# Order in which the first projection's sums are finished and read, their PSUM banks, and VectorE's order around the first attention scores, in a decoder layer on one core

## The chip, the core and the metric

The kernel runs on one core of one Trainium2 chip. The core has TensorE (PE; its weight loads are shown apart as PEld), VectorE (DVE), ScalarE (ACT), GpSimd (POOL) and SyncE (SP), which here only issues DMA transfers. Each engine works through its own queue in order and waits on semaphores of the others. Matmul results land in PSUM, which has eight banks; a 128x512 float32 tile fills one. The metric is the time of one execution in microseconds on the device; lower is better.

## The reference, cut to what matters

One layer of a decoder with 512 tokens and 1024 channels, all in float32:

```python
shift1, scale1, gate1, shift2, scale2, gate2 = split(silu(c) @ w_ada + b_ada, 6)
h = rmsnorm(x, norm1_g) * (1 + scale1) + shift1
qa, ka, va, qd, kd, vd, ga, gd = split(h @ w_in)          # 512, 128, 128, 512, 512, 512, 1024, 1024 columns
out_a = sliding_window_attention(qa, ka, va, sinks)       # 8 heads of 64, 2 key heads, window 128
out_d = differential_attention(qd, kd, vd)                # 4 heads
merged = sigmoid(ga) * (out_a @ w_branch_swa) + sigmoid(gd) * (out_d @ w_branch_diff)
x = x + gate1 * (merged @ w_out)
x = x + gate2 * conv_ffn(rmsnorm(x, norm2_g) * (1 + scale2) + shift2)
out = rmsnorm(x, final_g)
```

## The kernel before

Every operand of a matmul is split into a high part (rounded to the matmul's format by ScalarE, which also is the cast) and a low part (the rest, by VectorE). A product is three matmuls: high by high, high by low, low by high. Reading a finished sum out of PSUM, an *evacuation* (`evac`, L422), is the same pair of operations: ScalarE writes the high part, VectorE subtracts it and writes the low part. The bank is free when both have read it.

**First projection.** `mm_k(k, part)` (L323) multiplies k-tile k (of 8) of the normalised input with the 768 columns for qa, ka and va. The six sums `acc6` stand in six banks at once: 0 to 3 are the four pairs of query heads, 4 is ka, 5 is va, transposed. The banks come from tags: `f` has two, `s` three, `t` two, `v` one. Sums 0 and 1 have the two `f` banks, 2 to 4 the three `s` banks, 5 the `v` bank. Each of the three parts goes over all six sums in turn. Then the six are evacuated in the order 0 to 5 (L430 to L434), and va is transposed back by TensorE (L438) and evacuated (L441).

**Steps and fills.** After this the order of TensorE's queue is written out by hand, and TensorE is fed from two sides. `fill(n)` (L482) issues n *steps* of background projections: one step is one k-tile of one 128-column projection, three matmuls, and a projection has eight steps. The first six are q, k and v of differential heads 0 and 1 (tiles pq, pk, pw; one `f` bank each). Their weights come through `prefetch` (L477): a DMA into one of four `raw` buffers, ScalarE's cast w_h, VectorE's low part w_l (L115). `tick` counts the steps. Between the fills stand the parts of windowed attention, by pair of heads:

- `swa_scores(i, n0)` (L520): twelve matmuls into two `s` banks (sw), for two of the four query blocks, then four VectorE instructions that add the distance bias, write the scores to st and take the row maxima (L547).
- `swa_softmax(i)` (L552): negated maxima, eight exponentials on ScalarE, the row sums, and a scaling of st by VectorE (L570), first for one head of the pair, then for the other.
- `swa_transpose(i, j)` (L573): seven transposes of st into the two `t` banks (tp, L582), then evacuation to pTh and pTl.
- `swa_values(i)` (L589): the products with va, into the `v` bank.

`SWA_FILL` gives how many steps stand in each gap. The first three entries are the gaps before the first scores of pair 0, before its second scores, and after its softmax.

**Conditioning rows.** `ada_rows` (L734) computes the rest of `silu(c) @ w_ada` on VectorE, in rounds: a DMA of 512 KB into a `raw` buffer (ra) and two operations that add it, scaled, to the tile arow (L746, L748). One round is issued at every 8th step; four fill one arow.

**What sets the order.** TensorE's queue there is in the order of the text. The queues of VectorE, ScalarE, SP and POOL are ordered when the program is built, by a list planner that goes through estimated times: of the instructions that it takes to be ready it issues the one of highest priority. Priority is the order of the text; blocks in `tc.high_priority(offset=...)` move ahead by the offset. Score maxima, softmax and evacuations of tp have the offset HP = 100000, the conditioning rounds half of it. On the chip each queue keeps that order, ready or not.

Of the kernel before, what the change touches and what calls it, by code (L numbers as in the profile page):

```python
# [8 lines left out]
F32 = mybir.dt.float32  # L9
# [19 lines left out]
ST = 6  # L29
ADA_LAG = 1  # L30
ADA_EVERY = 8
ADA_START = 4
V_LAG = 13
STAT_LAG = 10
NORM_LAG = 16
SWA_FILL = (4, 2, 3, 2, 2, 2, 2, 3)
DIFF_FILL = (3, 2, 4, 2)
WARM = 14
GROUPS = ((0,), (1,), (2,), (3,), (4,), (5,), (6,), (7,))
# [13 lines left out]
def kernel(  # L53
# [170 lines left out]
    )  # L224
    nc.sync.dma_start(crow[0:66, :], conv_w[0].rearrange("t (a p) -> (t a) p", p=P))
    nc.sync.dma_start(crow[66:88, :], conv_b[0].rearrange("(a p) -> a p", p=P))
    acc6 = [fbank("a0"), fbank("a1"), sbank("a2"), sbank("a3"), sbank("a4"), vbank("a5")]
    man = ExitStack()
    man.enter_context(tc.manual_schedule(engines={nc.vector.engine, nc.scalar.engine, nc.tensor.engine}))
    cs = cpool.tile([P, 8], F32, name="cs")  # L230
# [91 lines left out]

    def mm_k(k, part):  # L323
        wh, wl = wts[k]
        lhs, rhs = ((wh, hTh), (wl, hTh), (wh, hTl))[part]
        for i in range(6):
            nc.tensor.matmul(
                acc6[i], lhs[:, i * P : (i + 1) * P], rhs[k],
                start=k == 0 and part == 0, stop=k == KT - 1 and part == 2,
            )  # L330


    def keep_warm(n):
# [93 lines left out]
            nc.scalar.activation(hi, src, AF.Copy, scale=scale)  # L427
            nc.vector.scalar_tensor_tensor(lo, src, scale, hi.bitcast(F32), ALU.mult, ALU.subtract)

    for i in range(4):  # L430
        evac(qa[:, i, 0], qa[:, i, 1], acc6[i], qsc[:, i : i + 1])
    evac(ka[:, 0], ka[:, 1], acc6[4])
    vT = ap.tile([P, S], F32, tag="tmp", bufs=2, name="vaT")
    nc.scalar.copy(vT, acc6[5])  # L434
    nc.gpsimd.memset(va.bitcast(F32), 0.0)
    pv = tbank("pva")
    for t in range(NT):
        nc.tensor.transpose(pv[:, t * P : (t + 1) * P], vT[:, t * P : (t + 1) * P], ident)  # L438
    pv3 = pv.rearrange("p (t d) -> p t d", t=NT)
    for a, cc in ((0, 0), (64, 192)):  # L440
        evac(va[:, 0, :, cc : cc + 64], va[:, 1, :, cc : cc + 64], pv3[:, :, a : a + 64])  # L441


    pcv = tbank("pcv", (P, 88))
# [37 lines left out]
    def fill(n):  # L482
        for _ in range(n):
            if not current:
                prefetch()
                if loaded:
                    wts, run = loaded.pop(0)
                    current.append(run(wts))
                    prefetch()
            if current:  # L490
                try:
                    next(current[0])
                except StopIteration:
                    current.clear()
            for e in list(later):
                e[0] -= 1
                if e[0] <= 0:
                    later.remove(e)
                    e[1]()
            tick[0] += 1  # L500
            if tick[0] >= ADA_START and tick[0] % ADA_EVERY == 0:
                next(ada, None)
# [17 lines left out]
    def swa_scores(i, n0):  # L520
        if n0 == 0:
            c = pairs[i] = Pair()
            c.mx, c.nm, c.lsum, c.es = (
                ap.tile([P, 2, NT], F32, tag=t, bufs=2, name=f"{t}{i}") for t in ("mx", "nm", "lsum", "es")
            )
            c.sb = [ap.tile([P, 2, P], F32, tag="st0", bufs=2, name=f"st{i}_0")]
            c.sb += [ap.tile([P, 2, 256], F32, tag="st", bufs=ST, name=f"st{i}_{n}") for n in range(1, NT)]
            c.pT = []
        c = pairs[i]
        sps = [sbank(f"sw{i}_{n0}_{j}", (P, 2, 256)) for j in range(2)]  # L530
        for n in (n0, n0 + 1):
            w = P if n == 0 else 2 * P
            k0 = max(0, n - 1) * P
            qs, ks = slice(n * P, (n + 1) * P), slice(k0, k0 + w)
            mm3_rows([
                (
                    sps[j][:, n - n0, :w],
                    [qa[64 * j : 64 * j + 64, i, b, qs] for b in range(2)],
                    [ka[64 * j : 64 * j + 64, b, ks] for b in range(2)],
                )  # L540
                for j in range(2)
            ])
        for n in (n0, n0 + 1):
            w = P if n == 0 else 2 * P
            for j in range(2):
                with tc.high_priority(offset=HP):
                    nc.vector.tensor_tensor_reduce(  # L547
                        c.sb[n][:, j, :w], sps[j][:, n - n0, :w], dsw[:, 256 - w : 256], 1.0, -3e38, ALU.add, ALU.max,
                        c.mx[:, j, n : n + 1],
                    )  # L550
# [183 lines left out]
    def ada_rows():  # L734
        for idx in range(4):
            for hf in range(2):
                c0 = (2 + idx) * D + hf * S
                ac = big.tile([P, S], F32, tag="sq2", name=f"arow{idx}{hf}")
                for k in range(0, KT, 2):
                    r = raw_tile([P, 2, S], f"ra{idx}{hf}_{k}")  # L740
                    nc.sync.dma_start(r, wada[k * P : (k + 2) * P, c0 : c0 + S].rearrange("(a p) n -> p a n", p=P))
                    with tc.high_priority(offset=HP // 2):
                        for a in range(2):
                            cc = cs[:, k + a : k + a + 1]
                            if k + a == 0:
                                nc.vector.tensor_scalar_mul(ac, r[:, a], cc)  # L746
                            else:
                                nc.vector.scalar_tensor_tensor(ac, r[:, a], cc, ac, ALU.mult, ALU.add)  # L748
# [46 lines left out]
    add_head(1)  # L795
    fill(SWA_FILL[0])
    swa_scores(0, 0)
    fill(SWA_FILL[1])
    swa_scores(0, 2)
    swa_softmax(0)  # L800
    fill(SWA_FILL[2])
    for i in range(SWA_PAIRS):
        more = i + 1 < SWA_PAIRS
        if more:
# [968 lines left out]
```

## Time and profile before

| | us |
|---|---|
| three runs | 717.43, 718.32, 718.40 |
| median | 718.32 |
| the profiled execution | 719.43 |
| its span from first to last instruction | 717.4 |

The span is what the views of the profile divide; about 2 us of the execution's time lie around it. The columns of the views are explained where they are shown. A row of a timeline is start and duration in us, engine, line of the kernel, operation, output and inputs, their shape, how many of them were merged into the row, and in brackets how long the engine had stood idle before it and what released it. Matmul durations overlap: from one start to the next is what a matmul costs in a row. The mean granted TensorE clock of the execution is 0.995 of full speed.

### The profile page before, as it was taken

The page shows a single profiled execution, that of the slowest core. Times are in us where ns is not written, and L with a number is a line of the kernel's source. Part 1 is how long each engine was busy: PE and PEld are TensorE (multiplying, and loading weights), DVE is VectorE, ACT ScalarE, POOL GpSimd, SP SyncE. Part 2 cuts the span into 40 slices and gives each one's busy share as a digit, 9 for nine tenths or more (in the row PEclk, how much of TensorE's full clock was granted, in tenths as well). Part 3 has the DMA queues.
Part 4 walks back from the last instruction along what each step waited for, and adds up shares of the span by engine and source line. Part 5 has one row for each costly group of instructions (what it writes and reads, how often), then busy time and mean ns, then how long its engine had stood idle before and what let it go on. Part 6 is the DMA issues. An engine that isn't in the chain of part 4 may idle for free. (4 is left out here: it accounts for less than half of the span.)

```text
span 717.4 us, 11279 instructions
## 1 busy us (share of the span) xinstructions
PE 690.6 (96%) x4187; PEld 603.1 (84%) x4187; DVE 588.9 (82%) x1125; ACT 383.6 (53%) x677; POOL 84.0 (12%) x101
## 2 busy tenths in 40 slices
PE   5998899999999999999999999999999999999995
PEld 5776788877887888888879999999999999888884
DVE  5998877887986674875379999888889899979996
ACT  4643656455554233432358665556555666655664
POOL 4000000000100110000012021111111101540300
PEclk9999999999999999999999999999999999999998
DMA  9986122534544565726817689878779738997903
GB/s 310 301 251 205 60 59 61 176 110 126 176 114 151 183 195 182 233 90 211 245 52 156 157 179 210 200 187 219 190 191 230 168 121 237 183 203 194 161 0 118
DMA packets 115863, 121.82 MB, mean 170 GB/s; under 512 B 4415, under 2 KB 93280, under 8 KB 115808
## 3 DMA queue, kind: packets, MB, share of 16 engines
q1 hardware_dynamic: 96894, 95.09, 41.7%
q0 software_dynamic: 18720, 25.73, 21.4%
q8 instruction: 33, 0.54, 0.3%
q10 hardware_dynamic: 194, 0.28, 0.1%
q14 instruction: 22, 0.18, 0.1%
HBM read 118.97 MB, written 2.11 MB: 169 GB/s over the span
## 5 line engine op out<-in xcount | busy, mean ns | idle before, releaser
L1112 PE MATMUL up<-t,m_whi 128*128 128x256 f32 x528 | 96.1, 283 | 0.0
L1112 PEld LDWEIGHTS up<-t,m_whi 128*128 128x128 f32 x528 | 82.3, 192 | 0.0
L1112 PE MATMUL up<-t,m_wlo 128*128 128x256 f32 x264 | 74.7, 283 | 0.1
L1112 PE MATMUL up<-bh,p_wlo 128*128 128x256 f32 x232 | 65.7, 284 | 0.7 <-DVE p_wlo L1055 0.7
L1112 PE MATMUL up<-bh,p_whi 128*128 128x256 f32 x232 | 65.6, 283 | 0.0
L1112 PE MATMUL up<-bl,p_whi 128*128 128x256 f32 x232 | 65.6, 283 | 0.0
L1112 PEld LDWEIGHTS up<-t,m_wlo 128*128 128x128 f32 x264 | 50.6, 192 | 0.3 <-DVE m_wlo L1055 0.3
L1112 PEld LDWEIGHTS up<-bh,p_wlo 128*128 128x128 f32 x232 | 44.4, 192 | 1.1 <-DVE p_wlo L1055 1.1
L1112 PEld LDWEIGHTS up<-bl,p_whi 128*128 128x128 f32 x232 | 44.5, 192 | 0.0
L1112 PEld LDWEIGHTS up<-bh,p_whi 128*128 128x128 f32 x232 | 44.5, 192 | 0.0
L748 DVE SCALAR_TENSOR_TENSOR arow<-ra,cs,arow 128x512 f32<-128x512 f32 x56 | 41.9, 748 | 3.0 <-DMA ra<-in_w_ada_dram 2.3
L1023 POOL DMA_DIRECT2D s<-in_w_up_dram x21 | 27.2, 1385 | 143.2 <-DMA s<-in_w_up_dram 61.0
L1055 DVE TENSOR_TENSOR m_wlo<-s,m_whi 128x1024 fp32r<-128x1024 f32 x31 | 37.8, 1220 | 2.0 <-ACT m_whi L1051 2.0
L1051 ACT CAST m_whi<-s 128x1024 fp32r<-128x1024 f32 x31 | 32.4, 1046 | 9.4 <-DVE s L1045 6.0
L1112 PE MATMUL up<-t,p_whi 128*128 128x256 f32 x176 | 32.2, 283 | 0.0
L174 POOL TENSOR_TENSOR r<-ms,mhalf 128x1 f32<-128x1 f32 (+1 forms) x16 | 13.1, 820 | 143.2 <-DVE ms L172 76.5
L678 ACT ACTIVATE sd<-sd,dmx 128x128 f32<-128x128 f32 (+3 forms) x32 | 17.8, 557 | 22.1 <-DVE dmx L676 15.3
L761 POOL DMA_DIRECT2D mod_rows<-arow x8 | 4.3, 540 | 205.2 <-ACT arow L760 205.1
L1112 PEld LDWEIGHTS up<-t,p_whi 128*128 128x128 f32 x176 | 27.4, 192 | 0.2 <-issue 0.2
L1119 ACT ACTIVATE gT<-a,cv 128x512 f32<-128x512 f32 x22 | 17.7, 813 | 17.7 <-DVE a L1154 17.3
L1051 ACT CAST p_whi<-wa 128x1024 fp32r<-128x1024 f32 x18 | 18.7, 1040 | 12.0 <-PE up L1112 9.0
L1112 PE MATMUL up<-t,p_wlo 128*128 128x256 f32 x88 | 24.9, 283 | 0.0
(485 smaller groups left out, 2119.3 us busy)
## 6 DMA issues: line engine op xcount, KB each, us to landing
ra<-in_w_ada_dram SPq DMA_DIRECT2D x32, 512.0 KB, 4.0
wa<-in_w_up_dram SPq DMA_DIRECT2D x22, 512.0 KB, 4.3
s<-in_w_up_dram SPq DMA_DIRECT2D x21, 512.0 KB, 4.9
s<-in_w_up_dram POOLq DMA_DIRECT2D x21, 512.0 KB, 7.3
adaw<-in_w_ada_dram SPq DMA_DIRECT2D x16, 512.0 KB, 5.3
w<-in_w_in_dram SPq DMA_DIRECT2D x12, 512.0 KB, 3.9
a<-in_w_up_dram SPq DMA_DIRECT2D x11, 512.0 KB, 4.9
b<-in_w_down_dram SPq DMA_DIRECT2D x10, 512.0 KB, 3.8
```

The lines of the kernel that those rows point to most:

```text
L174: nc.gpsimd.tensor_tensor(r0, ms, mhalf[:, :n], ALU.pow)
L678: nc.scalar.activation(pm[m], pm[m], AF.Exp, bias=mx[:, m : m + 1], scale=slope, accum_out=lsum[:, m : m + 1])
L748: nc.vector.scalar_tensor_tensor(ac, r[:, a], cc, ac, ALU.mult, ALU.add)
L761: nc.gpsimd.dma_start(mod_rows[idx : idx + 1, hf * S : (hf + 1) * S], row)
L1023: nc.gpsimd.dma_start(dst, upblock(*blk), accum_op=ALU.add)
L1051: nc.scalar.copy(W[J, name][0], R[J, SRC[name]])
L1055: nc.vector.tensor_sub(lo, R[J, SRC[name]], hi.bitcast(F32))
L1112: nc.tensor.matmul(o[u], w[:, k, cu], b[:, k], start=name in ("p1", "m5", "p2") and k == 0 and x == 0, stop=k == 3 and x == 2, skip_group_ ...
L1119: nc.scalar.activation(grow(j), av[J][:, u], AF.Identity, bias=cv[:, 66 + j : 67 + j], scale=cv[:, 44 + j : 45 + j])
```

## The change

- **Banks and order of the sums.** The sums are finished, and their banks taken, in the order 0, 4, 2, 5, 1, 3. Sums 0 and 1 keep `f` banks; 4, 2 and 5 (ka, query pair 2, va) have the `s` banks, and 3 (query pair 3) has the `v` bank.
- **One by one.** In the last k-tile, parts 1 and 2 are issued together for each sum.
- **Evacuation.** Sums 0, 4, 2, 5, 1 are evacuated in this order. Sum 3 and the turning of va (`turn_va`) come after the first softmax and one step.
- **VectorE's order.** `tc.issue_after(ins)` makes every instruction that its block traces on the engine of `ins` come after `ins` in that engine's queue; it adds no wait for a result. The steps between the two score groups of pair 0, and its second scores, come behind the maxima of the first scores. The softmax of pair 0, the steps around it, the evacuation of sum 3 and of va come behind the maxima of the second scores.
- **Weights.** The third weight (v of head 0) is requested in the eighth step, no longer in the first.
- **Conditioning rounds** up to step 20 lose their raised priority: those of steps 8 and 16.
- **Steps.** Of the nine steps around the first scores, 2, 2 and 5 stand in the three gaps, before 4, 2 and 3.

```diff
@@ -29,11 +29,12 @@
 ST = 6
 ADA_LAG = 1
 ADA_EVERY = 8
+ADA_EASY = 20
 ADA_START = 4
 V_LAG = 13
 STAT_LAG = 10
 NORM_LAG = 16
-SWA_FILL = (4, 2, 3, 2, 2, 2, 2, 3)
+SWA_FILL = (2, 2, 5, 2, 2, 2, 2, 3)
 DIFF_FILL = (3, 2, 4, 2)
 WARM = 14
 GROUPS = ((0,), (1,), (2,), (3,), (4,), (5,), (6,), (7,))
@@ -224,7 +225,9 @@
     )
     nc.sync.dma_start(crow[0:66, :], conv_w[0].rearrange("t (a p) -> (t a) p", p=P))
     nc.sync.dma_start(crow[66:88, :], conv_b[0].rearrange("(a p) -> a p", p=P))
-    acc6 = [fbank("a0"), fbank("a1"), sbank("a2"), sbank("a3"), sbank("a4"), vbank("a5")]
+
+    DONE = (0, 4, 2, 5, 1, 3)
+    acc6 = {i: (fbank, sbank, vbank)[(0, 0, 1, 2, 1, 1)[i]](f"a{i}") for i in DONE}
     man = ExitStack()
     man.enter_context(tc.manual_schedule(engines={nc.vector.engine, nc.scalar.engine, nc.tensor.engine}))
     cs = cpool.tile([P, 8], F32, name="cs")
@@ -322,12 +325,15 @@
 
     def mm_k(k, part):
         wh, wl = wts[k]
-        lhs, rhs = ((wh, hTh), (wl, hTh), (wh, hTl))[part]
-        for i in range(6):
-            nc.tensor.matmul(
-                acc6[i], lhs[:, i * P : (i + 1) * P], rhs[k],
-                start=k == 0 and part == 0, stop=k == KT - 1 and part == 2,
-            )
+        last = k == KT - 1
+        if last and part == 2:
+            return
+        for i in DONE:
+            for p in (1, 2) if last and part else (part,):
+                lhs, rhs = ((wh, hTh), (wl, hTh), (wh, hTl))[p]
+                nc.tensor.matmul(
+                    acc6[i], lhs[:, i * P : (i + 1) * P], rhs[k], start=k == 0 and p == 0, stop=last and p == 2
+                )
 
 
     def keep_warm(n):
@@ -427,18 +433,25 @@
             nc.scalar.activation(hi, src, AF.Copy, scale=scale)
             nc.vector.scalar_tensor_tensor(lo, src, scale, hi.bitcast(F32), ALU.mult, ALU.subtract)
 
-    for i in range(4):
+    nc.gpsimd.memset(va.bitcast(F32), 0.0)
+
+    def evac_q(i):
         evac(qa[:, i, 0], qa[:, i, 1], acc6[i], qsc[:, i : i + 1])
+
+    evac_q(0)
     evac(ka[:, 0], ka[:, 1], acc6[4])
+    evac_q(2)
     vT = ap.tile([P, S], F32, tag="tmp", bufs=2, name="vaT")
     nc.scalar.copy(vT, acc6[5])
-    nc.gpsimd.memset(va.bitcast(F32), 0.0)
-    pv = tbank("pva")
-    for t in range(NT):
-        nc.tensor.transpose(pv[:, t * P : (t + 1) * P], vT[:, t * P : (t + 1) * P], ident)
-    pv3 = pv.rearrange("p (t d) -> p t d", t=NT)
-    for a, cc in ((0, 0), (64, 192)):
-        evac(va[:, 0, :, cc : cc + 64], va[:, 1, :, cc : cc + 64], pv3[:, :, a : a + 64])
+    evac_q(1)
+
+    def turn_va():
+        pv = tbank("pva")
+        for t in range(NT):
+            nc.tensor.transpose(pv[:, t * P : (t + 1) * P], vT[:, t * P : (t + 1) * P], ident)
+        pv3 = pv.rearrange("p (t d) -> p t d", t=NT)
+        for a, cc in ((0, 0), (64, 192)):
+            evac(va[:, 0, :, cc : cc + 64], va[:, 1, :, cc : cc + 64], pv3[:, :, a : a + 64])
 
 
     pcv = tbank("pcv", (P, 88))
@@ -486,7 +499,10 @@
                 if loaded:
                     wts, run = loaded.pop(0)
                     current.append(run(wts))
-                    prefetch()
+                    if tick[0]:
+                        prefetch()
+            if tick[0] == 7:
+                prefetch()
             if current:
                 try:
                     next(current[0])
@@ -544,7 +560,7 @@
             w = P if n == 0 else 2 * P
             for j in range(2):
                 with tc.high_priority(offset=HP):
-                    nc.vector.tensor_tensor_reduce(
+                    c.last = nc.vector.tensor_tensor_reduce(
                         c.sb[n][:, j, :w], sps[j][:, n - n0, :w], dsw[:, 256 - w : 256], 1.0, -3e38, ALU.add, ALU.max,
                         c.mx[:, j, n : n + 1],
                     )
@@ -739,7 +755,7 @@
                 for k in range(0, KT, 2):
                     r = raw_tile([P, 2, S], f"ra{idx}{hf}_{k}")
                     nc.sync.dma_start(r, wada[k * P : (k + 2) * P, c0 : c0 + S].rearrange("(a p) n -> p a n", p=P))
-                    with tc.high_priority(offset=HP // 2):
+                    with tc.high_priority(offset=HP // 2) if tick[0] > ADA_EASY else ExitStack():
                         for a in range(2):
                             cc = cs[:, k + a : k + a + 1]
                             if k + a == 0:
@@ -795,10 +811,15 @@
     add_head(1)
     fill(SWA_FILL[0])
     swa_scores(0, 0)
-    fill(SWA_FILL[1])
-    swa_scores(0, 2)
-    swa_softmax(0)
-    fill(SWA_FILL[2])
+    with tc.issue_after(pairs[0].last.ins):
+        fill(SWA_FILL[1])
+        swa_scores(0, 2)
+    with tc.issue_after(pairs[0].last.ins):
+        swa_softmax(0)
+        fill(1)
+        evac_q(3)
+        turn_va()
+        fill(SWA_FILL[2] - 1)
     for i in range(SWA_PAIRS):
         more = i + 1 < SWA_PAIRS
         if more:
```

## The prediction

> **What bounds the kernel now.** I read the page first, then busy time by stage, then what TensorE waited for, and last the order of instructions on each engine in the one stage where it waited.
>
> ```profile
> span 717.4 us, 11279 instructions
> ...
> PE 690.6 (96%) x4187; PEld 603.1 (84%) x4187; DVE 588.9 (82%) x1125; ACT 383.6 (53%) x677; POOL 84.0 (12%) x101
> ```
>
> ```profile
> 60.28:72.00 11.72, 9.38 (x49) 6.76 (x49) 8.54 (x22) 3.06 (x7) 0.00 (x0) 0.85 0.72 227
> 72.00:82.20 10.20, 8.03 (x49) 5.68 (x47) 9.96 (x37) 7.33 (x24) 0.00 (x0) 1.00 0.31 104
> 82.20:135.00 52.80, 52.80 (x347) 44.75 (x347) 41.78 (x132) 31.47 (x93) 0.70 (x1) 1.00 0.27 81
> ```
>
> The columns of the second view are the stretch, its length, then busy time (and instructions) of PE, PEld, DVE, ACT and POOL, the granted clock, the DMA share and GB/s. TensorE is the bound. From 82.2 to 135 us it never rests; between 60.28 and 82.20 us, where the first projection hands over to attention, it is idle for 2.34 + 2.17 us and is granted 0.85 of its clock in the first half. The waits to 260 us say for whom it rests:
>
> ```profile
> PE sw L125 <- DVE qa L428: 1.6, 2, 1.0
> PE td L693 <- DVE sd L684: 1.6, 3, 1.1
> ...
> PE tp L582 <- DVE pTl L425: 1.2, 1, 1.2
> ...
> PE tp L582 <- DVE st L570: 1.0, 1, 1.0
> ...
> PE od L119 <- DVE aTl L425: 0.5, 1, 0.5
> PE pq L118 <- DVE qa L428: 0.5, 1, 0.5
> ...
> PE sw L125 <- DVE ka L425: 0.3, 1, 0.3
> ```
>
> Everything named qa, ka, st or pTl here lies between 60.28 and 82.20 us and ends on a DVE instruction. TensorE's own order there (start, duration, line, instruction, in brackets the idle time before it):
>
> ```profile
> 57.32 1.56 PE L327 MATMUL a<-hThB,w0l 128*128 128x512 f32 x6
> 58.72 1.56 PE L327 MATMUL a<-hTlB,w0h 128*128 128x512 f32 x6
> 60.74 0.50 PE L118 MATMUL pq<-hThA,w_h 128*128 128x512 f32 x1 [0.46 <-DVE qa L428]
> ...
> 64.97 0.33 PE L125 MATMUL sw<-ka,qa 64*128 64x128 f32 x1 [0.62 <-DVE qa L428]
> 66.29 0.32 PE L125 MATMUL sw<-ka,qa 64*128 64x128 f32 x1 [1.00 <-DVE qa L428]
> 66.89 0.84 PE L125 MATMUL sw<-ka,qa 64*128 64x128 f32 x10 [0.27 <-DVE ka L425]
> ...
> 70.15 1.59 PE L125 MATMUL sw<-ka,qa 64*128 64x256 f32 x12
> ...
> 73.94 0.96 PE L125 MATMUL sw<-ka,qa 64*128 64x128 f32 x12
> 74.82 0.50 PE L118 MATMUL pk<-hThA,w_h 128*128 128x512 f32 x1
> ...
> 77.45 1.14 PE L582 MATMUL tp<-ident,st 128*128 128x128 f32 x7 [0.97 <-DVE st L570]
> ...
> 81.18 1.01 PE L582 MATMUL tp<-ident,st 128*128 128x128 f32 x7 [1.20 <-DVE pTl L425]
> 82.13 0.97 PE L125 MATMUL sw<-ka,qa 64*128 64x256 f32 x12
> ```
>
> And VectorE's, with two rows of ScalarE behind it:
>
> ```profile
> 56.48 0.69 DVE L321 TENSOR_TENSOR hTlB<-hf,hThB 128x512 fp32r<-128x512 f32 x1
> 57.09 2.35 DVE L115 TENSOR_TENSOR w_l<-w,w_h 128x1024 fp32r<-128x1024 f32 x2
> 59.36 0.48 DVE L746 TENSOR_SCALAR arow<-ra,cs 128x512 f32<-128x512 f32 x1
> 59.93 0.75 DVE L428 SCALAR_TENSOR_TENSOR qa<-a,qsc,qa 128x512 fp32r<-128x512 f32 x1
> ...
> 63.50 0.75 DVE L748 SCALAR_TENSOR_TENSOR arow<-ra,cs,arow 128x512 f32<-128x512 f32 x1 [1.49 <-DMA ra<-in_w_ada_dram]
> ...
> 66.15 0.68 DVE L425 TENSOR_TENSOR ka<-a,ka 128x512 fp32r<-128x512 f32 x1
> ...
> 71.78 0.42 DVE L547 CUSTOM_DVE_ANT_0 st<-sw,dsw 128x256 f32<-128x256 f32 x1 [1.69 <-PE sw L125]
> ...
> 77.03 1.07 DVE L570 TENSOR_SCALAR st<-st,lsum 128x128 f32<-128x128 f32 x4
> ...
> 80.45 1.15 DVE L425 TENSOR_TENSOR pTl<-tp,pTh 128x512 fp32r<-128x512 f32 x2
> ```
>
> ```profile
> 59.21 2.42 ACT L427 ACTIVATE qa<-a,qsc 128x512 fp32r<-128x512 f32 x4 [1.83 <-PE a L327]
> ...
> 73.18 1.05 ACT L114 CAST w_h<-w 128x1024 fp32r<-128x1024 f32 x1 [4.95 <-PE pq L119]
> ```
>
> The conditioning rows (arow, L746/L748), which nobody needs for another 40 us, are interleaved with the evacuation of the projection. At 63.50 one of them stands in VectorE's queue waiting 1.49 us for its weights, with qa 2, qa 3 and ka behind it. ka, which every score needs, is done only at 66.83.
>
> **The change, step by step.** A *step* is one k-tile of a projection: three 512-wide matmuls. Six start in 1.40 us (57.32 to 58.72), 0.233 us each, so a step is 0.70 us.
>
> *Sums finished one by one.* The number of matmuls is the same. In the last k-tile the low-weight and low-activation products are issued accumulator by accumulator. That tile's 18 matmuls start at 57.32 − 1.40 = 55.92; a0 is complete after the 8th instead of the 13th, at 55.92 + 7 × 0.233 + 0.40 = 57.95 instead of 59.12, the others each 0.47 later, a3 at the old end. The 8th needs hTlB, which is ready at 57.17 and was used only at 58.72; 0.4 us of cover are left, and if they were gone the whole tail would slip by the lateness, as no other work stands between.
>
> *Evacuation.* ScalarE takes 0.57 to 0.60 us each (four in 2.42): a0 58.05, a4 58.6, a2 59.2, vaT 59.8, a1 60.4. VectorE still splits one early weight from 57.09 to 58.23 (half of the 2.35 row; the second is deferred), then has no arow in the way: a0's low part to 59.3, ka's to 59.9, a2's to 60.6, a1's to 61.6, at 0.67 and 0.60 each. The last projection matmul starts at 59.88, so the first pq can start at 60.11, on a0's bank, free since 59.3: the 0.46 goes. Two steps last until 61.5. The first scores need qa 0 (59.3), ka (59.9) and two of the three score banks, which now held a4, a2, a5 (free at 59.9, 60.6, 60.4). So 0.62 + 1.00 + 0.27 go too: together **2.35 us**, with 0.9 us of cover (61.5 − 60.6).
>
> *The clock.* Busy time of PE, granted clock, DMA share and GB/s in two smaller stretches:
>
> ```profile
> 68.30:71.70 3.40, 3.40 (x18) 0.52 0.67 188
> ...
> 76.40:82.20 5.80, 3.63 (x23) 1.00 0.54 184
> ```
>
> Right behind those three waits the clock is 0.52 for 3.40 us: 3.40 × 0.48 = **1.6 us**. Without the waits I expect none of it. The second stretch rests longer (2.17 us) and keeps 1.00, so the dip is not certain to follow or to stay away; bounds 0 and 1.6. [...]
>
> *Restarts.* A 512-wide matmul shows 0.40 to 0.50 us alone (1.56 less five starts of 0.233; the 60.74 row) against 0.233 in a row, so each of the six stops hides about 0.15 beyond its idle figure; four go: **0.6** (bounds 0 and 1.0).
>
> *First maxima ahead, and the fills moved.* Edges that only order VectorE's queue cost no instruction. The nine steps around the first two score groups are now 2, 2, 1 + 4 instead of 4, 2, 3. The maxima start when the group has ended (71.78 after 70.15 + 1.59), and the first scaled probabilities come 77.03 + 1.07 = 78.10, or 6.4 us after it. In that time TensorE had 3 + 2 steps and a score group; now 1 + 4 + 2 steps (4.9), a score group (74.82 − 73.94 = 0.88), the four value transposes (about 0.45 by the score group's pitch) and some 0.3 of switching: 6.5 us. So the 0.97 goes. The 1.20 came from pTl starting at 80.45, 1.9 us after transposes that ended at 78.59, because VectorE was still scaling the other half; as TensorE now arrives later in that chain I expect 0.3 to 0.5 left. Of 2.17 I take **1.7** (bounds 0 and 2.17). In the same place ScalarE may or may not put a 1.05 cast ahead of the exponentials again, as at 73.18: that is inside the bounds.
>
> *What is deferred.* Four conditioning rounds ran before 82.2:
>
> ```profile
> L748 DVE SCALAR_TENSOR_TENSOR arow<-ra,cs,arow 128x512 f32<-128x512 f32 x7 | 5.2, 746 | 1.5 <-DMA ra<-in_w_ada_dram 1.5
> ```
>
> Now the rounds of steps 8 and 16 lose their priority, and 24 and 32 follow them because they add to the same tile. About six of these eight operations (6 × 0.746 = 4.5 us) and a 1.2 us weight split move into the time after the second score group of pair 1. There VectorE is busy 41.78 of 52.80 us; with 5.7 more, 90%. Most fits the gaps while ScalarE does exponentials, but one operation ahead of a pTl or a score maximum makes TensorE wait up to its own 0.75. I take **−0.7** (bounds 0 and −2.5). POOL's zeroing of va moves in the text, but POOL is idle in all these stretches: nothing. One more switch between kinds of matmul: **−0.1**.
>
> On SP the third weight is asked for in the 8th step instead of the first; nothing lies between them in that queue. Its raw slot, though, and that of the first conditioning round are now held until VectorE reaches them after the second maxima, so the loads behind, above all the fifth and sixth weight (first used in steps 33 and 41), are issued later; for these see the rival of a late weight.
>
> *Sum:* 2.35 + 1.6 + 0.6 + 1.7 − 0.7 − 0.1 = **5.45 us**. The profiled execution took 719.43 us with its span of 717.4, so 2.0 lie around the span; it would become 714.0. It is 1.1 above the median of the runs, 718.32, and a saving in the middle of a stage that TensorE bounds passes through to the end whole: 718.32 − 5.45 = 712.9 us. All gains at their upper bound and no deferred cost: 2.35 + 1.6 + 1.0 + 2.17 − 0.1 = 7.0, or 711.3.
>
> **Rivals.** *The deferred rows collide (chance 0.18).* Pairs 1 to 3 have six places where TensorE waits for pTl or maxima with little room. For it: 90% load, and rounds 24 and 32 still carry a high priority. Against: between 82.2 and 135 TensorE did not wait at all. One operation ahead at each, 0.6 of its 0.75 showing: 6 × 0.6 = 3.6 in place of 0.7, a gain of 2.55: 715.8 us.
>
> *The scores still wait (0.10).* The change doesn't do what it says: ScalarE or VectorE takes a weight's cast or split between the evacuations, because the planner thinks it has the time. For it: just that happened at 57.09 and 73.18. 1.22 us less the 0.9 of cover is 0.3 of new wait, but if two such pieces come, about 1.5 us of waits and with them the clock dip stay: 5.45 − 1.5 − 1.6 = 2.35, or 716.0 us.
>
> *Slower: a weight comes late (0.09).* SP waited like this before:
>
> ```profile
> SPq L464 <- DVE w_l L115: 16.8, 2, 16.1
> ```
>
> ```profile
> w<-in_w_in_dram SPq DMA_DIRECT2D x12, 512.0 KB, 3.9
> ```
>
> If the load of the fifth weight is issued less than 3.9 + 1.05 + 1.22 = 6.2 us before step 33, TensorE stands for what is missing. Issued only as that step starts, it costs 6.2 and a clock dip of 1.6: 5.45 − 7.8 = −2.35, or 720.7 us. It turns the sign where more than 3.9 us of it show. Against: the second maxima should end near 66 us, and step 33 comes 20 steps of 0.70 after the second score group of pair 1, so at 75 + 14 = 89 us at the earliest.
>
> *Nothing gained in the end (0.05).* The planner orders the later queues anew, and the waits after 135 us (the td and od rows, 2.1 us) grow by as much as the front gains: 718.3 us.
>
> **How the numbers follow.** Forecast 0.58: 712.9 us, its own range 711.0 to 714.9 (the bounds of clock, restarts, transposes and deferral, not all at once). The range for 8 in 10 runs from 710.8 to 717.0: it takes in the first two rivals and leaves out slower, no change, and the tails. A measurement of this kernel can tell about 0.2%, 1.4 us. Faster by more: 0.58 + 0.18 + 0.10 less a little of their tails, 0.83; slower: 0.10; within: 0.07.
>
> **What would show it.** Right: the first pq starts near 60.1 with no wait; no wait for qa or ka at the first scores; granted clock 1.00 from 60 to 80; the first score group of pair 0 near 61.5, the second of pair 1 near 75 instead of 82.13; arow operations spread from about 66 to 110. Wrong: a wait for st or pTl of over 1 us in pair 0; new waits of TensorE for pTl, sw or w_l between 75 and 128; a clock below 1.00 there; a wait for a weight near step 33. If the score group comes 7 us earlier and the time falls by much less, the loss is after 75 us, and the stage table will say where.

## The result, and the profile after

| | before | after | after / before |
|---|---|---|---|
| median of 9 runs each, us | 718.38 | 716.06 | 0.9968 (95%: 0.9953 to 0.9982) |
| the profiled execution, us | 719.43 | 716.59 | |
| its span, us | 717.4 | 714.5 | |
| its mean granted clock | 0.995 | 0.993 | |

The kernel became 2.3 us faster (0.32%; by the interval 1.3 to 3.4), where 5.45 had been forecast.

The first page of the changed kernel, and its busy time by stage, in the same columns as before (stretch, length, PE, PEld, DVE, ACT, POOL, granted clock, DMA share, GB/s):

```profile
span 714.5 us, 11275 instructions
...
PE 688.4 (96%) x4187; PEld 603.0 (84%) x4187; DVE 588.5 (82%) x1125; ACT 384.2 (54%) x677; POOL 84.4 (12%) x101
```

```profile
0.00:18.00 18.00, 9.54 (x55) 9.18 (x56) 10.71 (x40) 7.08 (x13) 8.10 (x26) 0.92 0.92 307
...
60.28:72.00 11.72, 11.72 (x76) 8.92 (x75) 9.27 (x34) 6.80 (x25) 0.00 (x0) 1.00 0.27 87
72.00:82.20 10.20, 8.11 (x54) 6.68 (x53) 9.97 (x33) 4.92 (x11) 0.00 (x0) 1.00 0.42 127
82.20:135.00 52.80, 51.99 (x335) 43.28 (x333) 44.75 (x132) 32.22 (x92) 0.70 (x1) 1.00 0.40 121
```

TensorE is still the bound. In the first half of the stage, 60.28 to 72 us, TensorE now never rests, and its clock is 1.00 where it had been 0.85. The second half is no better than it was: idle 10.20 − 8.11 = 2.09 us, before 2.17. Behind 82.2 us there are 0.81 us of idle where there were none. And the clock is below full in another place, in the first 18 us (0.92).

The first row of what TensorE waited for up to 260 us (in total, times, longest), and its order around the change:

```profile
PE tp L598 <- DVE pTl L431: 2.9, 2, 2.1
```

```profile
60.49 0.39 PE L334 MATMUL a<-hTlB,w0h 128*128 128x512 f32 x1
60.72 0.40 PE L119 MATMUL pq<-hThA,w_h 128*128 128x512 f32 x1
...
62.20 0.95 PE L126 MATMUL sw<-ka,qa 64*128 64x128 f32 x12
...
72.06 0.60 PE L598 MATMUL tp<-ident,st 128*128 128x128 f32 x4
74.76 0.55 PE L598 MATMUL tp<-ident,st 128*128 128x128 f32 x3 [2.09 <-DVE pTl L431]
...
77.39 0.97 PE L126 MATMUL sw<-ka,qa 64*128 64x256 f32 x12
...
91.68 1.01 PE L598 MATMUL tp<-ident,st 128*128 128x128 f32 x7 [0.81 <-DVE pTl L431]
```

The first pq follows the last projection matmul by 0.23 us, the pitch of matmuls in a row; the first scores have no wait. In this stretch all waits named qa, ka and st are gone. What is left there is one new wait of 2.09 us *inside* the first seven transposes of pair 0, after four of them, and one of 0.81 us in pair 1. These rows of VectorE and ScalarE lie behind them:

```profile
60.03 0.68 DVE L431 TENSOR_TENSOR ka<-a,ka 128x512 fp32r<-128x512 f32 x1
...
74.01 0.69 DVE L431 TENSOR_TENSOR pTl<-tp,pTh 128x512 fp32r<-128x512 f32 x1
74.62 0.42 DVE L431 TENSOR_TENSOR va<-pva,va 128x256 fp32r<-128x256 f32 x1
...
90.33 0.69 DVE L116 TENSOR_TENSOR arl<-arow,arh 128x512 fp32r<-128x512 f32 x1
90.94 1.15 DVE L431 TENSOR_TENSOR pTl<-tp,pTh 128x512 fp32r<-128x512 f32 x2
```

```profile
67.07 0.37 ACT L430 CAST va<-pva 128x256 fp32r<-128x256 f32 x1 [4.87 <-PE pva L451]
67.34 0.30 ACT L575 ACTIVATE es<-nm,sink 128x4 f32<-128x4 f32 x1
...
71.37 0.19 ACT L578 ACTIVATION_READ_ACCUMULATOR st<-st,nm 128x1 f32 x1
71.46 0.35 ACT L430 CAST va<-pva 128x256 fp32r<-128x256 f32 x1
...
72.20 1.03 ACT L115 CAST w_h<-w 128x1024 fp32r<-128x1024 f32 x1
73.14 0.58 ACT L430 CAST pTh<-tp 128x512 fp32r<-128x512 f32 x1
```

ka is done at 60.71, which had been 66.83: no conditioning row stands between the evacuations any more.

Seven transposes need both `t` banks: four matmuls in one, three in the other. At 72.06 one `t` bank is still held by the turned va (pva, transposed at 66.38). va is read in two halves. The first half's cast runs at 67.07. The second stands in ScalarE's queue behind all eight exponentials of the softmax (67.34 to 71.56) and runs at 71.46; its low part on VectorE comes only at 74.62. So the last three transposes cannot go to va's bank, which is read until 74.62 + 0.42 = 75.04. They start at 74.76, as soon as pTl has freed the bank that the first four had filled (74.01 + 0.69 = 74.70). The wait is put down to pTl, and truly so, but the bank that is missing is va's.

As at 73.18 before, a weight's cast (72.20) has run ahead of pTh, but pTh is over by 73.72, before VectorE comes to pTl.

In pair 1, arl (L116, 0.69 us, the low part of the finished conditioning row) stands right ahead of the pTl that TensorE needs at 90.87: that is the deferred work showing.

### The profile page after: what moved, and what is told of

It reads as the page before. It is cut to its first block, busy times and chain, and to the rows that moved or that the text cites. A ratio compares the mean times of both kernels' runs of the same rounds, so it can differ in the third digit from the quotient of the medians.

```text
span 714.5 us, 11275 instructions
## 1 busy us (share of the span) xinstructions
PE 688.4 (96%) x4187; PEld 603.0 (84%) x4187; DVE 588.5 (82%) x1125; ACT 384.2 (54%) x677; POOL 84.4 (12%) x101
```

## Experiments

The ratios are to the kernel before, run on the same chip in the same batch. Diffs are to the changed kernel unless another is named.

**va's evacuation ahead (e1).** The new wait is taken at its suspected cause: the casts of va go ahead of the exponentials.

```diff
+            with tc.high_priority(offset=2 * HP):
+                evac(va[:, 0, :, cc : cc + 64], va[:, 1, :, cc : cc + 64], pv3[:, :, a : a + 64])
```

> The changed kernel, with the two evacuations of the turned va (ScalarE's casts and VectorE's low parts) at a priority above the softmax. Theory: in the changed kernel TensorE waits 2.09 us before the fifth transpose of pair 0, because the second of the two t banks is still held by the turned va, whose second cast stands behind all eight exponentials (71.46) and whose low part is done at 75.04. With both casts ahead of the exponentials that wait is gone (under 0.4 us), the second score group of pair 1 starts 1.7 to 2.1 us earlier behind the last projection matmul, and the time falls from about 716.1 to 714.0 to 714.6. Rival: the bank was not what it waited for, and pTl itself is late because VectorE is busy with softmax and maxima: then the wait stays above 1 us and the time at 715.5 to 716.5.

Measured: 713.47 us (before 717.69), ratio 0.9936 (0.9915 to 0.9958). TensorE:

```profile
70.64 0.93 PE L599 MATMUL tp<-ident,st 128*128 128x128 f32 x7
...
73.89 1.01 PE L599 MATMUL tp<-ident,st 128*128 128x128 f32 x7 [0.94 <-DVE pTl L431]
...
89.64 1.01 PE L599 MATMUL tp<-ident,st 128*128 128x128 f32 x7 [1.34 <-DVE pTl L431]
```

All seven transposes run in one go at 70.64. Of the 2.09 us, 0.94 come back at the second group of pair 0, which was hidden behind the larger wait, and pair 1's wait is 1.34 in place of 0.81. The theory held, but not its sizes: the second score group of pair 1 starts 74.83 − 59.11 = 15.7 us behind the last projection matmul in place of 16.9, so 1.2 us earlier and not 1.7 to 2.1, and yet the median lies below the 714.0 expected.

**va in another bank, order unchanged (e9).** e1 also moves work on ScalarE and VectorE. Here only the bank is another.

```diff
-        pv = tbank("pva")
+        pv = sbank("pva")
```

> The changed kernel with the turned va in an s bank, one of three, of which the score groups of that time use two, and no longer in a t bank; the order of its two casts and all priorities stay as changed, its second cast still behind the exponentials. Theory (it is the bank): both t banks are free for the first transposes of pair 0, all seven go without the wait of 2.09 us, and only the wait for pTl before the second half is left, 0.9 as with va first; the time is 713.5 to 715.0, 1 to 2.5 us below the changed kernel. Rival (it is the order on ScalarE and VectorE that made va early worth something): the wait stays above 1.5 us in all and the time is 715.4 to 716.4.

Measured: 713.29 us (before 717.92), ratio 0.9941 (0.9921 to 0.9961).

```profile
59.90 0.40 PE L119 MATMUL pq<-hThA,w_h 128*128 128x512 f32 x1
...
71.23 0.93 PE L598 MATMUL tp<-ident,st 128*128 128x128 f32 x7
...
73.94 1.01 PE L598 MATMUL tp<-ident,st 128*128 128x128 f32 x7 [0.40 <-DVE pTl L431]
74.88 0.97 PE L126 MATMUL sw<-ka,qa 64*128 64x256 f32 x12
...
89.77 1.01 PE L598 MATMUL tp<-ident,st 128*128 128x128 f32 x7 [1.39 <-DVE pTl L431]
```

```profile
68.59 0.28 ACT L575 ACTIVATE es<-nm,sink 128x4 f32<-128x4 f32 x1
...
70.64 0.35 ACT L430 CAST va<-pva 128x256 fp32r<-128x256 f32 x1
```

va's second cast still comes last (70.64, behind both heads' exponentials, the second head's from 68.59), and the wait inside the first transposes is gone all the same. Up to pTl, ScalarE and VectorE work in the same order as in the changed kernel. It was the bank that was missing, not the order of the casts by itself.

**The sums alone (e2), the order alone (e3)**, both built from the kernel before.

```diff
+    DONE = (0, 4, 2, 5, 1, 3)
...
+    evac_q(0)
     evac(ka[:, 0], ka[:, 1], acc6[4])
+    evac_q(2)
...
+    evac_q(1)
+    evac_q(3)
```

That was e2, which also takes `acc6` and `mm_k` from the change and turns va at once. e3 keeps the sums, their banks and `SWA_FILL` as they were, and requests the third weight as the change does:

```diff
+ADA_EASY = 20
...
+    with tc.issue_after(pairs[0].last.ins):
+        fill(SWA_FILL[1])
+        swa_scores(0, 2)
+    with tc.issue_after(pairs[0].last.ins):
+        swa_softmax(0)
+        fill(SWA_FILL[2])
```

> The kernel before with the first part of the change alone: banks, order of the sums, one by one in the last k-tile, evacuation in the new order; VectorE's order, conditioning priority, third weight and step counts as before. Theory (the waits of the front come from the conditioning rows in VectorE's queue, the banks only from the order): the wait of the first pq goes (0.46), but one row in the queue still waits for its load near 63 us and holds the evacuations behind it; of the 1.9 us that TensorE waited for qa and ka at the first scores 0.3 to 1.0 is left, the transposes wait as before. Time 716.6 to 718.0. Rival: finishing the sums one by one and reading ka second is what gives the gain: waits at the first scores under 0.3 us and the time at 715.5 to 716.5, like the changed kernel.

> The kernel before with the second part alone: first maxima ahead of other VectorE work, conditioning rounds of steps 8 and 16 without raised priority, third weight in the eighth step; banks, order of the sums, evacuation and step counts (4, 2, 3) as before. Theory: with no row in the way the five low parts follow each other from 59.9, 0.66 us each, ka is done near 63.3, before TensorE comes to the first scores near 64.0, so the 1.9 us go and with them the dip of the clock; the first pq still waits 0.4. Time 715.0 to 716.5, that is, most of the gain of the whole change comes from this part. Rival: sums finished together are the bound, ka comes late all the same, waits at the first scores above 0.8 us and the time at 717.3 to 718.5.

Measured: e2 715.73 us, ratio 0.9971 (0.9956 to 0.9985); e3 715.8, ratio 0.9970 (0.9957 to 0.9983). Each part alone gives as much as both together; e2 is faster than its theory, and its rival held, while e3's theory held. Their waits at the first pq and the first transposes:

```profile
60.00 0.50 PE L118 MATMUL pq<-hThA,w_h 128*128 128x512 f32 x1 [0.26 <-DVE qa L432]
...
74.00 1.22 PE L591 MATMUL tp<-ident,st 128*128 128x128 f32 x7 [1.25 <-DVE st L579]
```

```profile
60.65 0.50 PE L119 MATMUL pq<-hThA,w_h 128*128 128x512 f32 x1 [0.46 <-DVE qa L429]
...
73.24 1.23 PE L586 MATMUL tp<-ident,st 128*128 128x128 f32 x7 [0.87 <-DVE st L574]
```

In neither do the first scores wait: earlier sums bring qa and ka in time, and so do evacuations without conditioning rows between them. Ahead of the first transposes both still wait for st. The 1.89 us of waits at the first scores, the largest term, are removed by either part, so the two gains do not add. Nor does either part have the changed kernel's wait of 2.09 us: both still turn va in the first steps. All waits of TensorE from the first pq to 135 us come to 4.52 us before, 2.51 in e2, 3.06 in e3 (1.33 of it for pTl in pair 1) and 2.90 in the changed kernel.

**Parts of the last k-tile together again (e7).** The old loop of `mm_k` in the new order of sums.

```diff
-            for p in (1, 2) if last and part else (part,):
...
+            nc.tensor.matmul(
+                acc6[i], lhs[:, i * P : (i + 1) * P], rhs[k],
```

> The changed kernel, but in the last k-tile each of the three parts goes over all six sums in turn again; banks and the order of evacuation as changed. Theory: a0 is complete 1.2 us later, so the first pq waits 0.3 to 0.6 for its low part, and the first scores still find ka and two banks in time, since the evacuation has 0.9 us of cover there. Time 0.3 to 0.8 above the changed kernel: 716.3 to 716.9. Rival: the whole chain of evacuations shifts by 1.2 us, the first scores and all behind wait as well, and the time is 717.0 to 717.8.

Measured: 715.82 us (before 717.37), ratio 0.9974 (0.9962 to 0.9986). The first pq waits 0.46 us again, the scores do not wait. Finishing the sums one by one is worth that 0.46; the time cannot tell it from the changed kernel, and it is below the 716.3 to 716.9 that were expected.

**Conditioning rows raised again (e4; with e1's edit: e5).**

```diff
-ADA_EASY = 20
+ADA_EASY = 0
```

> The changed kernel with the raised priority for every conditioning round again (the edges that hold them behind the second maxima stay). Theory: in the changed kernel rows put off into the softmax of pair 1 make the low part of the scores and pTl late near 91 us, where TensorE waits 0.81; with the rows done earlier that wait is under 0.3, but they now stand between softmax and pTl in pair 0, whose wait grows from 2.1 to 2.5 or more. Time within 0.7 us of the changed kernel, 715.5 to 716.8. Rival: the deferral costs more than that one wait, and the time falls to 715.0 or less.

> The kernel with va's evacuations first, and the raised priority for every conditioning round again. With va first two waits are left, both before the second half of a pair's transposes and both for pTl: 0.94 in pair 0, 1.34 in pair 1; in pair 1 a conditioning row stands right ahead of pTl. Theory: with the rows raised they are done by pair 0, so the 1.34 goes as the 0.81 did when only the rows were raised, and the 0.94 stays or grows by at most one row (0.75). Time 712.4 to 713.6. Rival: the rows only move the loss, pair 0 then waits 2 us or more, and the time is 713.5 to 714.8.

Measured: e4 716.18 us (before 717.69), ratio 0.9967 (0.9953 to 0.9981); e5 713.1 (before 717.37), ratio 0.9943 (0.9928 to 0.9957). e5 waits 1.00 us in pair 0 and 0.61 in pair 1, in sum 0.67 less than e1 (the 1.34 was expected to go whole); their medians, 713.1 and 713.47 in different batches, differ by less than they scatter. In e4 the wait inside the transposes grew to 2.77 us and no wait is left in pair 1:

```profile
74.78 0.84 PE L598 MATMUL tp<-ident,st 128*128 128x128 f32 x3 [2.77 <-DVE pTl L431]
```

```profile
72.00:82.20 10.20, 7.43 (x39) 6.04 (x39) 9.00 (x33) 2.65 (x6) 0.00 (x0) 0.83 0.53 156
82.20:135.00 52.80, 52.80 (x341) 44.30 (x339) 44.81 (x131) 33.63 (x96) 0.70 (x1) 1.00 0.37 111
```

So the wait in pair 1 does belong to the deferred rows, and taking the deferral back costs about as much in pair 0 (2.77 − 2.09 = 0.68). Its row also shows the clock at 0.83 right behind the 2.77 us.

**Steps moved between the halves of the transposes (e6).** e1, and in every pair two steps more between the two halves of its transposes, one fewer on each side of the next softmax.

```diff
-SWA_FILL = (2, 2, 5, 2, 2, 2, 2, 3)
+SWA_FILL = (2, 2, 5, 2, 4, 1, 1, 3)
```

> The kernel with va's evacuations first, and in every pair two of the background steps moved: four instead of two between the two halves of the transposes, one instead of two on each side of the next softmax. Theory: the waits for pTl (0.94 and 1.34) are a matter of cover, and two steps more, 1.4 us, hide both; pairs 2 and 3 had no wait and stay so. Time 710.8 to 712.2. Rival: TensorE then reaches the next half's values or transposes too early and waits there for what it no longer waits for here: 713.0 to 714.2.

Measured: 713.13 us, ratio 0.9944 (0.9925 to 0.9964). The theory fell, the rival held. The wait in pair 0 is gone and 0.92 is left in pair 1, but pairs 2 and 3, now short of steps, wait 0.3, 0.3 and 0.2.

**The waits filled with matmuls (e8, e13).** To try whether the idle time is what lowers the clock, without touching any other work, eight matmuls whose result nobody reads are put into the wait: e8 ahead of the first scores of the kernel before, e13 between the two halves of the changed kernel's first transposes.

```diff
+    spare = vbank("spare")
+    for _ in range(8):
+        nc.tensor.matmul(spare, onesr, hTh[0], start=True, stop=True)
```

> The kernel before with eight extra 512-wide matmuls (1.87 us, into the free v bank, never read) right ahead of the first scores, where TensorE waits 1.9 us in any case. They add work but should add no time: TensorE is only kept busy. Theory: the dip of the clock (0.52 for 3.4 us in the profile of the kernel before) follows the idle time and comes in part of the executions only; filled, no execution has it there: granted clock 1.00 from 60 to 76 us, the slowest executions of the kernel before (719 to 721) vanish, and the median falls by 0.4 to 1.2 us, to 716.5 to 717.3. Rival: the dip is not due to this idle time, or it costs nothing at the end: median and spread like the kernel before, 717.4 to 718.4.

> The changed kernel with eight extra 512-wide matmuls (1.87 us, into the free v bank, never read) between the two halves of the first transposes, right where TensorE waits 2.1 us. No wait is taken away; TensorE is only kept busy in it. Theory (the clock): the wait itself costs the changed kernel about 1 us against the kernels with va first, and the rest of their 2.6 us is the dip of the clock that follows a wait of that length in most executions. Filled, the time falls though work is added: median 713.8 to 715.2, the slowest below 716, mean granted clock 0.995 or more in most executions. Rival: the clock has no part in it, the wait of 2.1 us is the whole difference, and the time stays at 715.5 to 716.6.

Measured: e8 719.36 us, ratio 1.0029 (1.002 to 1.0038); e13 714.53 (before 717.24), ratio 0.9972 (0.9961 to 0.9982). Both leave the price of the clock open. In e8 the clock was 1.00 from 60 to 76 us, but the planner ordered VectorE anew and the waits moved (1.11 us inside the first scores of pair 1, 1.66 before the first transposes); the time is outside both ranges expected. In e13 the wait inside the transposes is down to 0.23 us. Its median is 1.3 to 1.5 us below the changed kernel's in the other batches, but the kernel before was lower beside it too, and the ratio is the changed kernel's. The three executions of the changed kernel beside it, without the extra matmuls (e14 to e16 below), took 713.45 to 713.98 us, less than e13's median, so no gain of the filling is shown.

**The same two kernels once more (e10, e11: before; e12, e14 to e16: changed).** No edit; each is another profiled execution, to see where the clock falls.

> The kernel before once more, for its profile. Theory: the waits of the front are the same to 0.1 us in each execution (0.46 before the first pq, 1.9 at the first scores, 2.2 at the transposes of pair 0), but the dip of the clock behind them is not: with the clock at 1.00 from 60 to 76 us the execution takes 716 to 717.7, with a dip 718 to 720. Rival: the dip is there every time, at the same place.

> The kernel before a third time, for its profile: as for the second.

> The changed kernel once more, beside the others on the same chip. Theory: the waits of 2.09 (pair 0) and 0.81 (pair 1) are there again, while the 0.4 and 0.5 us that its first profile lost against the kernel before near 200 and 370 us, and the dip of the clock near 16 us, need not be. Time 715.5 to 716.5, 1.2 to 2.5 us below the kernel before. Rival: the later losses belong to the change and come back within 0.2 us each.

> The changed kernel once more, for the place of the clock's dip. Theory: an execution of 715.5 or more has a stretch of half clock, either behind the wait of 2.1 us (72 to 80 us) or in the start (14 to 20 us); one of 713.5 to 714.5 has none before the end. Rival: executions of 716 have no dip, and the difference is elsewhere.

> The changed kernel a further time, for the place of the clock's dip: as above.

> The changed kernel a further time, for the place of the clock's dip: as above.

Measured: e10 716.12 and e11 717.2; e12 715.85 as the median of 12 (713.66 in the profiled execution; ratio 0.9969, 0.9955 to 0.9983); e14, e15, e16 713.98, 713.45, 713.73. Below are the 3.40 us that hold the waits at the first scores and the 3.40 behind them, first in the execution of before on which the prediction rests, then in e10, where the same work runs 1.0 us earlier:

```profile
64.90:68.30 3.40, 2.06 (x14) 1.51 (x15) 3.40 (x7) 0.37 (x1) 0.00 (x0) 0.97 0.47 141
68.30:71.70 3.40, 3.40 (x18) 2.39 (x16) 1.79 (x11) 0.00 (x0) 0.00 (x0) 0.52 0.67 188
```

```profile
63.90:67.30 3.40, 2.13 (x15) 1.61 (x16) 3.40 (x6) 0.38 (x1) 0.00 (x0) 1.00 0.53 165
67.30:70.70 3.40, 3.40 (x24) 2.55 (x23) 3.21 (x21) 0.12 (x1) 0.00 (x0) 1.00 0.58 171
```

The same kernel, nearly the same waits at the first scores (1.89 and 1.74 us), TensorE busy 2.06 and 2.13 us of 3.40: once the clock drops to 0.52 behind them, once it stays. e11, which waits 1.51 us at the first scores, keeps 1.00 there as well and has its dip at the start of the program instead (0.91 over the first 18 us, 0.57 from 14 to 18):

```profile
0.00:18.00 18.00, 11.07 (x58) 10.71 (x59) 10.46 (x41) 6.99 (x14) 8.13 (x26) 0.91 0.92 312
...
60.28:72.00 11.72, 9.79 (x56) 7.04 (x56) 10.13 (x32) 3.81 (x8) 0.00 (x0) 1.00 0.70 227
```

Of the five profiled executions of the changed kernel, two (the first and e14) dip at the start, both to 0.72 over 14 to 20 us; e12, e15 and e16 show 1.00 in every stretch up to 700 us. e14 goes against its theory, which had no dip in an execution of 713.5 to 714.5 us. It also shows that a dip at the start can cost little: its first pq starts at 59.48, and at 59.20 to 59.47 in the three without. The only profiled execution of the changed kernel above 715.5 us, the first, dips at the start. The waits of 0.24 us near 198 and 1.34 near 369 in the changed kernel's first profile are not there in e12, as was expected; the change does not cause them.

## Why the prediction missed its size

The direction was right; the gain was less than half of that forecast. Two steps of the sum failed by about 1.6 us each: the clock, and the first maxima with the moved fills. That the time lies in the range is luck, as the range reached up to 717.0 only for the first two rivals, and neither happened as described. e10 against e12 is the comparison that reads the steps best, since both show a clock of 1.00 in every stretch up to 700 us: 716.12 − 713.66 = 2.46 us.

```profile
57.77 1.56 PE L327 MATMUL a<-hTlB,w0h 128*128 128x512 f32 x6
59.80 0.50 PE L118 MATMUL pq<-hThA,w_h 128*128 128x512 f32 x1 [0.47 <-DVE qa L428]
...
63.87 0.32 PE L125 MATMUL sw<-ka,qa 64*128 64x128 f32 x1 [0.47 <-DVE qa L428]
65.19 0.33 PE L125 MATMUL sw<-ka,qa 64*128 64x128 f32 x1 [1.00 <-DVE qa L428]
65.79 0.84 PE L125 MATMUL sw<-ka,qa 64*128 64x128 f32 x10 [0.27 <-DVE ka L425]
...
74.95 1.13 PE L582 MATMUL tp<-ident,st 128*128 128x128 f32 x7 [1.07 <-DVE st L570]
...
78.60 1.01 PE L582 MATMUL tp<-ident,st 128*128 128x128 f32 x7 [1.12 <-DVE pTl L425]
79.54 0.97 PE L125 MATMUL sw<-ka,qa 64*128 64x256 f32 x12
```

```profile
59.47 0.40 PE L119 MATMUL pq<-hThA,w_h 128*128 128x512 f32 x1
...
73.53 0.55 PE L598 MATMUL tp<-ident,st 128*128 128x128 f32 x3 [2.12 <-DVE pTl L431]
...
76.17 0.98 PE L126 MATMUL sw<-ka,qa 64*128 64x256 f32 x12
...
90.39 1.01 PE L598 MATMUL tp<-ident,st 128*128 128x128 f32 x7 [0.74 <-DVE pTl L431]
```

- **Sums and evacuation, 2.35 us: right.** In e10 these four waits are 0.47 + 0.47 + 1.00 + 0.27 = 2.21; in the changed kernel all four are gone. Only, e2 and e3 show that the scores' share is not the sums' alone.
- **Clock, 1.6 us: failed.** The dip seen behind these waits was taken for their consequence. e10 and e11 have the waits without it (1.00 from 60 to 80 us). In the first profile it did cost about that: from the start of the last projection matmul to the second score group of pair 1 it takes 82.13 − 59.88 = 22.25 us, e10 20.60. But the changed kernel's first execution, which dips at the start, reaches the stage 60.49 − 59.88 = 0.61 us later. What the waits change can at most be how often a dip falls, and by the mean granted clock (more on it below) the change gained nothing there: its median is 0.994 over e12's twelve executions and over the seventeen of before beside them.
- **Restarts, 0.6 us: undersized.** From the start of the last projection matmul to the second score group of pair 1, e10 takes 79.54 − 58.94 = 20.60 us (58.94 is the last of six starts 0.233 apart from 57.77). e12 takes 76.17 − 59.24 = 16.93; its last projection matmul is one pitch before the first pq at 59.47. Of the 3.67 us gained, 2.21 are the waits above and 2.19 − 2.12 = 0.07 the transposes'; about 1.4 stand in no bracket. A part is legible: from 63.87 to 65.19 is 1.32 us, of which 1.00 is idle and 0.07 a score matmul's pitch (0.88 for twelve), so that stop cost 0.25 more than its idle figure; the one at 65.79 as much, and pq's, the one at 63.87 and the two ahead of transposes 0.16 to 0.17 each, by the start of the matmul ahead of them (58.94, 63.01, 73.49, 77.08). The six come to 1.16 us, and the changed kernel keeps one stop. The rest of the 1.4 has no name.
- **First maxima ahead, and the fills moved, 1.7 of 2.17 us: this step failed; 0.07 came of it.** It is the main error of the argument. The st wait did go. "As TensorE now arrives later in that chain I expect 0.3 to 0.5 left" is what did not come true: 2.09 us (2.12 in e12). I had read the old 1.20 as a late pTl and asked only when pTl would come, not which banks the transposes need and who holds them. The change moves va's turning from the first steps (61.74 in e10) into the softmax (65.14 in e12), so one of two `t` banks is out of use just when the first transposes want both. e1 and e9 remove this in two different ways and both run at 713.3 to 713.5 us, in e9's batch 715.85 − 713.29 = 2.56 us below the changed kernel. With the bank free and all else unchanged, e9 leaves 0.40 us, within the 0.3 to 0.5 expected; e1, which also moves work, leaves 0.94.
- **Deferred rows, −0.7 us: right.** 0.81 in the first profile, 0.74 in e12, plus a restart. e4 shows that they are its cause.
- **Switch, −0.1 us:** not to be told apart from the rest; **the median as base:** the profiled executions of one kernel differ by more than the gain (before: 719.43, 716.12, 717.2), so a sum made against one of them carries that.

Together, without dips: 2.21 + 0.07 + 1.4 − 0.74 − 0.15 (its restart) = 2.8, and the changed execution reached the stage 0.3 us later (59.24 against 58.94): 2.5, the 2.46 measured.

Of the rivals, the collision of the deferred rows came in pair 1 alone, once and not six times. That the scores still wait fell. So did the late weight: no wait of TensorE up to 260 us ends on one. The measured time, 716.06, is near that of the first two rivals (715.8 and 716.0), but by a mechanism that was not among them.

**Open.** Why e9 and e1 are 2.56 us and not some 1.0 us below the changed kernel. By waits, e12's front has 1.7 us more than e9's (16.93 against 74.88 − 59.67 = 15.21, counted as above) and its pair 1 has 0.65 less. That makes 1.05 us and leaves 1.5. The mean granted clock of each execution bears on these. It also counts the idle end, where the clock is 0.50 in the two traces of which that part was read (from 713.3 us to the end in before, from 707.9 in the first of the changed kernel), so one step of it proves little; but the four traces at 0.996 or 0.997 that were read to 700 us (e10, e12, e13, e15) have no dip up to there, and the six with one have 0.993 to 0.995 (e16, at 0.995, has none). Of e12's twelve executions nine lie at 0.994 or below (715.09 to 717.21 us) and two at 0.996 (713.66 and 713.80); of e9's six one lies so low (0.992, 715.3 us) and four at 0.996 or 0.997 (712.39 to 713.32). At the upper clock the two kernels are thus 0.86 us apart in the mean (713.73 against 712.87), about what the waits say, and most of the rest goes with a lower clock in most executions of the changed kernel. Whether the wait of 2.09 us brings that about stays open: e13, with the wait filled, still has seven of twelve executions at 0.994 or below, and none of the changed kernel's five traces has a dip behind the wait (1.00 from 72 to 80 us in each). e4's 0.83 behind its 2.77 us wait is one instance, not proof.

## What to carry over

A tile that is moved later keeps its PSUM bank later: for every moved evacuation, list the tags it shares and who takes the next buffer. The releaser that a trace names for a wait need not be what made it necessary; here pTl was named and va's bank was missing. And a dip of the clock in one profiled execution is not a property of the kernel until a second execution shows it in the same place: here 0.52 over 3.40 us behind the first scores in one profiled execution of the kernel before, 1.00 there in two others. The best versions here turn va in a score bank, or evacuate it ahead of the softmax: 0.9936 to 0.9944 of the time before.

## What the runs showed of the hardware

In the two traces in which the clock's dip within the work was read to its edges, it is 0.50 for 3.40 us: from 68.16 to 71.56 us in before, from 14.98 to 18.38 in the first of the changed kernel. Four more have one: e11 and e9 (0.57 over 14 to 18 us in both), e14 (0.62 over the same stretch) and e4 (0.83 over 72 to 82.2). Where it comes differs from execution to execution of one kernel: in the kernel before, behind the first scores (before), at 14 to 18 us (e11) or nowhere up to 700 us (e10); in the changed one, near 15 to 18 us (the first, e14) or nowhere up to 700 us (e12, e15, e16). The idle time that the rows of before and e10 show does not settle it: TensorE was busy for 2.06 of the 3.40 us up to 68.30 in before, with the dip behind them, and for 2.13 of 3.40 in e10, without one. What sets it off, these runs do not show. Second, the six stops of TensorE in e10's stretch each cost 0.16 to 0.26 us beyond the idle time that the trace brackets, 1.16 in all, so several short waits weigh more than their sum.
